# Pads in eight pools of a decoder-layer kernel: the two operands of most matrix multiplications get equal addresses modulo 256 bytes

## The chip, the core and the metric

The kernel runs on one core of a Trainium2 chip. Its engines work side by side, each through a queue of its own: TensorE (PE in the profile, with PEld for its loads of the stationary operand), VectorE (DVE), ScalarE (ACT), GpSimd (POOL) and SyncE (SP), which here issues most transfers. They share an on-chip memory of 128 partitions, the SBUF; the results of matrix multiplications land in a second memory, the PSUM. The metric is the device time of one execution in microseconds, as a median of runs.

## The reference

One layer of a decoder with 512 tokens and a width of 1024, all in float32. In short:

```
hn = rms_norm(x, g_mix);  z = hn @ w_in            # queries, keys, values, pool inputs, gates
A  = trailing-window pooling mixer                 # @ w_pool_out
B  = sparse attention: compressed + selected + window branches, sigmoid gated   # @ w_nsa_out
C  = cross-attention into mem (256 rows)           # @ w_x_out
x  = x + (sigmoid(g0)*A + sigmoid(g1)*B + sigmoid(g2)*C) @ w_o
h  = rms_norm(x, g_ffn)
# PEER: 8 heads, each picks 16 of 128*128 one-neuron experts by two half-queries
s  = scores of h @ w_peer_q against sub_keys;  ids, gate = two-stage top-16, softmax
x  = x + sum_k gate_k * gelu(h . u[ids_k]) * v[ids_k]
out = rms_norm(x, g_final)
```

## The kernel before, in words

**Numbers.** Each float32 factor `a` is held as two tiles: `a_hi`, a copy of `a` in the format `fp32r`, and `a_lo = a - a_hi`. A product is the sum of three matmuls, hi·hi, hi·lo and lo·hi. `split` (L132 to L134) makes the pair: ACT copies to the hi tile, DVE or POOL subtracts for the lo tile.

**One matmul has two operands in SBUF.** The *stationary* operand (128 columns, one LDWEIGHTS in the profile) is loaded into TensorE; the *moving* operand (64 to 512 columns) is then streamed through it. The profile names them in the order moving, stationary: `z<-hnh,wh` streams `hnh` through `wh`. While one matmul streams, the load for the next one runs beside it.

**The stages, in order of time** (us from the start of the span):

1. 0 to 40: memory keys and values (`mh`, `ml` against weights; 256 columns).
2. 40 to 250: the columns of `w_in` in tiles of 128 (`mm3_steps`, L161: `hnh`, `hnl` are moving, 512 columns, the weight tile `wh` or `wl` stationary), the values (L416, 280 columns), cross-attention (L454, L489) and its merge (`oxh`, `oxl`).
3. 240 to 515: sparse attention (L894, L926, L942 to L951) in an order of units, with the pool merge (`poolh`, `pooll`) and the next keys and queries between them in pieces of four matmuls.
4. 515 to 587: merge of the attention output (`onh`, `onl` and again `hnh`, `hnl`; 512 columns). 587 to 634: the projection `w_o` (L1156; the weights are moving, `mgh`, `mgl` stationary).
5. 635 to 745: the PEER queries (`q_mm`, L161: `hfh`, `hfl` moving, all 512 tokens).
6. From 635 on, the first layer of the experts (`hidden`, L161: 128 blocks `j` of 128 experts). It streams only the tokens 160 to 511 of `hfh`, `hfl`, so 352 columns, 24 matmuls a block: `p[:, X:NT]`, `x[:, k, t0 + X:T]` with `t0 = 128`, `X = 32`. 72 blocks (`LEAD`) run ahead, up to 1070 us, beside the retrieval of the expert numbers and the one-hot matmuls of the gates (L1453); their results go out to device memory.
7. 1074 to 1822: the last layer of the experts (`experts`, L1611). An iteration is one block: the 128 rows of `v` (two halves of 512 columns, hi and lo) are moving, the gated hidden values `wgh`, `wgl` are stationary: 3 token blocks x 3 products x 2 halves = 18 matmuls of 512 columns. The first 56 iterations also hold the 24 matmuls of `hidden`; the last 72 take the stored results. Beside it the 128 remaining tokens are done row by row: POOL gathers 256 rows of `u` and `v` (L1476), DVE multiplies them (L1490, L1496).

**What sets the order.** The schedule is manual: each engine works in program order. `weave` merges the experts' generator with the gathering one by given costs, `tiles` does so for attention.

**Pools and addresses.** A pool is a stack of tiles. Left pools grow from low addresses up, right pools from the top down, in the order in which they are opened. Tiles lie one behind the other in the order of the calls, and each start is rounded to 32 bytes. A tile that nobody reads (`name="pad"`) only moves what lies behind it (in a right pool: all the tiles of the pool, and the pools under it). One such pad stands in the kernel before: `wv2.tile([128, 216], F32, name="pad")` ahead of the expert weights.

Of the kernel before, what the change touches and what calls it, by code (L numbers as in the profile page):

```python
# [10 lines left out]
F32 = mybir.dt.float32  # L11
F32R = mybir.dt.float32r
# [12 lines left out]
KD = 8  # L25
# [85 lines left out]
def layer(ctx: ExitStack, tc: tile.TileContext, A: dict, out: bass.AP, dbg=None):  # L111
    nc = tc.nc
    v, s, g, pe = nc.vector, nc.scalar, nc.gpsimd, nc.tensor
# [6 lines left out]
    def sbuf(stack, name, side="left"):  # L120
        return stack.enter_context(tc.tile_pool(name=name, bufs=1, side=side, reuse_waits="tile"))
# [147 lines left out]
    rp = sbuf(rst, "rp", "right")  # L269
    acc = rp.tile([128, KD, T], F32, name="acc")  # L270
    poolh = rp.tile([128, 4, T], F32R, name="poolh")
    pooll = rp.tile([128, 4, T], F32R, name="pooll")
    mgp = sbuf(rst, "mg", "right")
    pms = ExitStack()
    pm = gfeed.pool = sbuf(pms, "pm", "right")
    xst = ExitStack()
    xa = sbuf(xst, "xa", "right")
    oxh = xa.tile([128, 4, T], F32R, name="oxh")
    oxl = xa.tile([128, 4, T], F32R, name="oxl")
    x2st = ExitStack()  # L280
    xk = sbuf(x2st, "xk", "right")
    Kh = xk.tile([128, 4, M], F32R, name="Kh")
# [113 lines left out]
    wv = sbuf(vst, "wv")  # L396
    WV = {}

    def wv_fetch(br):
        raw = wv.tile([128, KD * 280], F32, tag="vr", name="vr")  # L400
        nc.sync.dma_start(raw, A["w_v"][br])
        WV[br] = raw

    def wv_part(br):
        hi = wv.tile([128, KD, 280], F32R, tag="vh", name="vh")
        lo = wv.tile([128, KD, 280], F32R, tag="vl", name="vl")
        split(hi, lo, WV[br].rearrange("p (k n) -> p k n", n=280), v)
        WV[br] = (hi, lo)

# [362 lines left out]
    kqp = sbuf(ast, "kq")  # L772
# [2 lines left out]
    SC = [kqp.tile([128, 2, 4, 32], F32, name=f"sc{qp}") for qp in range(2)]  # L775
    for t_ in SC:
        g.memset(t_, NEG)

    def compress(gq, qp):

        def job():
            p = psum("z", [128, T])
            pc = p.rearrange("p (q r i c) -> p q r i c", q=2, r=4, i=2)
            sc = SC[qp]
            ns = [7 + 8 * (2 * qp + qi) for qi in range(2)]
            t_ = {}

            def steps():
                for qi in range(2):
                    qb = 2 * qp + qi  # L790
                    for r in range(4):
                        pe.matmul(pc[:, qi, r], Q[gq, r][:, qb * 128:(qb + 1) * 128], KC[:, gq],
                                  start=qi == 0 and r == 0, stop=qi == 1 and r == 3, skip_group_check=True)
                yield 0.9

            def add0():
                for qi, n in enumerate(ns):
                    j0 = 31 - n
                    v.tensor_tensor(sc[:, qi, :, 0:n], pc[:, qi, :, 0, 0:n], TTC[:, gq * 4:gq * 4 + 4, j0:j0 + n], op=OP.add)

            def add1():
                for qi, n in enumerate(ns):
                    v.tensor_tensor(sc[:, qi, :, 0:n], sc[:, qi, :, 0:n], pc[:, qi, :, 1, 0:n], op=OP.add)

            def top():
                t_["m"] = kqp.tile([128, 2, 4], F32, name="cnm")
                v.tensor_reduce(t_["m"], sc, axis=AX.X, op=OP.max)

            def sub():
                t_["e"] = kqp.tile([128, 2, 4, 32], F32, name="cex", bufs=2)  # L810
                v.tensor_tensor(t_["e"], sc, t_["m"][:, :, :, None].to_broadcast([128, 2, 4, 32]), op=OP.subtract)

            def exp():
                s.activation(t_["e"], t_["e"], AF.Exp)

            def total():
                t_["s"] = kqp.tile([128, 2, 4], F32, name="csm")
                v.tensor_reduce(t_["s"], t_["e"], axis=AX.X, op=OP.add)

            def inverse():  # L820
                v.reciprocal(t_["s"], t_["s"])

            def gated():
                v.tensor_tensor(t_["s"], t_["s"], gsig[:, 2 * qp:2 * qp + 2, gq * 4:gq * 4 + 4], op=OP.mult)

            def scaled():
                v.tensor_tensor(t_["e"], t_["e"], t_["s"][:, :, :, None].to_broadcast([128, 2, 4, 32]), op=OP.mult)

            def turned():
                PcT = [kqp.tile([128, 384], F32R, name=f"PcT{i}") for i in range(2)]  # L830
                pt = psum("tr", [128, 4, 128])
                for qi in range(2):
                    pe.transpose(pt[:, 1 - qi], t_["e"][:, qi].rearrange("p r c -> p (r c)"), ident)
                split(PcT[0][:, 0:256], PcT[1][:, 0:256], pt[:, 0:2].rearrange("p q t -> p (q t)"))
                for i in range(2):
                    s.activation(PcT[i][:, 256:384], f(PcT[i])[:, 0:128], AF.Copy)
                PC[gq, qp] = PcT

            TURN[gq, qp] = turned
            return p, steps(), [add0, add1], [top, sub, exp, total, inverse, gated, scaled]  # L840
        return job
# [235 lines left out]
    ep = sbuf(ctx, "ep")  # L1077
# [2 lines left out]
    mbx = ep.tile([128, X], F32, name="mbx")  # L1080
    HG = [ep.tile([128, NT], F32, name=f"hg{i}") for i in range(6)]
    idle = list(HG)

    lead_q = [s]

# [12 lines left out]
    n2 = sbuf(n2s, "n2")  # L1098
# [2 lines left out]
    X1 = [*(x1g[:, b] for b in range(GB)), *(x1n[:, b] for b in range(ND))]  # L1101
    iota16 = n2.tile([128, 16], F32, name="iota16")
    gf = n2.tile([128, D], F32, name="gf")
    src = A["iota128"]
    loads = [lambda b=b: nc.sync.dma_start(X1[b], A["x"][b * 128:(b + 1) * 128]) for b in range(NB)]
    loads.append(lambda: bcast_row(gf, A["g_ffn"]))
# [365 lines left out]
    ex_ = []  # L1472
# [92 lines left out]
    def experts():  # L1565
        acc_o.extend(psum(("S", "S", "tr", "tr", "o", "o")[i], [128, 512]) for i in range(2 * ND))
        for n in range(-1, 128):
            m = n + 1
            if m < 128:
                j = order[m]  # L1570
                if j >= LEAD:
                    U[m] = feed.take(("u", j))
                vfetch(m + 3)
                hfetch(m + 4)
                if m == 8:
                    bcast_row(gl, A["g_final"])
                if m == 100:
                    for b in range(GB, NB):
                        X1[b] = (X1B if b == GB
                                 else uf.tile([128, D], F32, tag="wr", name="wr", bufs=2))  # L1580
                        nc.sync.dma_start(X1[b], x1d[b - GB])
                if m % 8 == 4 and m + 4 < 128:
                    gload(m // 8 + 1)
                if j >= LEAD:
                    vpart(m)
                    yield 1.35
                    H[m] = hidden(U.pop(m))
                gh = GH.pop() if GH else ex_[0].tile([128, NT], F32, name="gh", bufs=2)
                idle.append(H[m])
                v.tensor_tensor(gh.rearrange("p (g t) -> p g t", t=UT), G[m // 8][:, :, m % 8 // 2, :, m % 2],  # L1590
                                H.pop(m).rearrange("p (g t) -> p g t", t=UT), op=OP.mult)
                if j < LEAD:
                    yield 1.0
                wh = WGH.pop() if WGH else ex_[0].tile([128, NT], F32R, name="wgh", bufs=3)
                wl = ex_[0].tile([128, NT], F32R, name="wgl", bufs=3)
                split(wh, wl, gh)
                if j < LEAD:
                    vpart(m)
                V[m] = (wh, wl, V[m])
                if j >= LEAD:  # L1600
                    yield 1.35
            if n < 0 or n == 126:
                continue

            ends = n == 127
            for b in range(ND):
                for k, hs in [(k, (half,)) for half in range(2) for k in (126, 127)] if ends else [(n, range(2))]:
                    wh, wl, vw = V[k]
                    for i, (a, c) in enumerate(((wh, vw[0]), (wl, vw[0]), (wh, vw[1]))):
                        for half in hs:  # L1610
                            pe.matmul(acc_o[2 * b + half], a[:, b * 128:(b + 1) * 128], c[:, half],  # L1611
                                      start=k == 0 and i == 0, stop=k == 127 and i == 2)
                    if ends and k == 127:
                        closing(GB + b, hs[0])
                        if b and hs[0] == 0:
                            finish(GB + b - 1)
                        if b and hs[0]:
                            for half in range(2):
                                output(GB + b - 1, half)
            V.pop(n)  # L1620
# [83 lines left out]
    gath = seq(*[gathered(b) for b in range(GB)])  # L1704
    ost2.close()
    wv2 = sbuf(hst, "wv2")
    wv2.tile([128, 216], F32, name="pad")
    vfetch(0)
    vfetch(1)
    gload(0)  # L1710
# [13 lines left out]
    X1B = ex.tile([128, D], F32, name="x1b")  # L1724
    bound_x()
    vfetch(2)
    seen = ep.tile([128, 1], F32, name="seen")
    g.tensor_copy(G[0][:, 0], own)
    g.tensor_copy(seen, VR[2][:, 0:1])
    weave((experts(), 2.7 * (128 - LEAD) + 1.0 * LEAD), (gath, 268 * GB))  # L1730
    finish(NB - 1)
    for half in range(2):
# [88 lines left out]
```

## Time and profile before

| | |
|---|---|
| time, median of 3 runs | 1832.12 us (1831.17 to 1832.64) |
| the profiled execution | 1831.29 us, its span 1829.5 us |
| TensorE, busy | 1805.9 us (99%), 10088 matmuls |
| VectorE, busy | 1361.5 us (74%) |
| ScalarE, busy | 836.7 us (46%) |
| GpSimd, busy | 765.6 us (42%) |
| moved by DMA | 446.00 MB, mean 244 GB/s |

A line of the groups reads: line, engine, operation, output<-inputs, shapes, count, busy us and mean ns of one, idle time before it and what ended it. Matmuls are pipelined: the *mean ns of one* runs from its start to its modelled end and is longer than the distance from one start to the next. What the stream costs is that distance. It is read from the timeline, where equal neighbours stand in one row: a row's start minus the start of the row before it, over the count of the row before it.

### The profile page before, as it was taken

The page shows a single profiled execution, that of the slowest core. Times are in us where ns is not written, and L with a number is a line of the kernel's source. Part 1 is how long each engine was busy: PE and PEld are TensorE (multiplying, and loading weights), DVE is VectorE, ACT ScalarE, POOL GpSimd, SP SyncE. Part 2 cuts the span into 40 slices and gives each one's busy share as a digit, 9 for nine tenths or more (in the row PEclk, how much of TensorE's full clock was granted, in tenths as well). Part 3 has the DMA queues.
Part 4 walks back from the last instruction along what each step waited for, and adds up shares of the span by engine and source line. Part 5 has one row for each costly group of instructions (what it writes and reads, how often), then busy time and mean ns, then how long its engine had stood idle before and what let it go on. Part 6 is the DMA issues. An engine that isn't in the chain of part 4 may idle for free.

```text
span 1829.5 us, 27951 instructions
## 1 busy us (share of the span) xinstructions
PE 1805.9 (99%) x10088; PEld 1584.9 (87%) x10088; DVE 1361.5 (74%) x2813; ACT 836.7 (46%) x1476; POOL 765.6 (42%) x597
## 2 busy tenths in 40 slices
PE   8999999999999999999999999999999999999998
PEld 7988888888888888999999988988988988888886
DVE  5453157766543479999989858998988998888886
ACT  6434267776642433554554543333333333333334
POOL 4323555555633233312222035666666664333320
PEclk9999999999999999999999999999999999999999
DMA  6225622112223432477999899999999999999992
GB/s 222 91 81 181 223 88 65 58 53 58 64 89 110 163 127 86 144 232 248 353 331 343 269 359 409 403 375 378 380 358 361 378 372 365 369 369 364 384 345 102
DMA packets 157276, 446.00 MB, mean 244 GB/s; under 512 B 16049, under 2 KB 61825, under 8 KB 154450
## 3 DMA queue, kind: packets, MB, share of 16 engines
q1 hardware_dynamic: 88194, 262.96, 40.1%
q0 software_dynamic: 41968, 152.14, 22.4%
q10 hardware_dynamic: 26976, 29.12, 4.8%
q8 instruction: 79, 1.29, 0.3%
q14 instruction: 59, 0.48, 0.1%
HBM read 402.15 MB, written 47.26 MB: 246 GB/s over the span
## 4 chain that ended last, share of the span: by engine, by line
PE 85%; DVE 5%; DMA 4%; ACT 3%; issue 1%; POOL 1%; ACTq 0%; DVEq 0%; SPq 0%; POOLq 0%
PE z L161 44%; PE S L1611 9%; PE o L1611 9%; PE tr L1611 9%; DMA ug<-in_u_rows_dram,ids 2%; PE S L894 1%; PE tr L926 1%; PE S L1156 1%; PE o L942 1%; DMA gd<-stg 1%; ACT pr L907 1%; PE o L416 1%; PE o L1239 1%; DVE pr L904 1%; PE z L1156 1%
## 5 line engine op out<-in xcount | busy, mean ns | idle before, releaser
L133 ACT ACTIVATE wh<-wr 128x1024 fp32r<-128x1024 f32 (+2 forms) x365 | 372.3, 1025 | 187.6 <-PE o L1611 47.6
L161 PE MATMUL z<-hfh,wh 128*128 128x352 f32 (+1 forms) x1136 | 376.0, 333 | 2.0 <-ACT wh L133 2.0
L134 DVE TENSOR_TENSOR wl<-wr,wh 128x1024 fp32r<-128x1024 f32 (+1 forms) x256 | 307.5, 1218 | 93.1 <-ACT wh L133 92.0
L134 POOL TENSOR_TENSOR wl<-wr,wh 128x1024 fp32r<-128x1024 f32 (+2 forms) x109 | 239.7, 2200 | 321.6 <-ACT wh L133 275.5
L161 PE MATMUL z<-hfl,wh 128*128 128x352 f32 (+1 forms) x1136 | 373.0, 330 | 0.0
L1476 POOL DMA_INDIRECT ug<-in_v_rows_dram,ids x128 | 175.3, 1370 | 208.7 <-DVE x1g L1496 191.9
L1476 POOL DMA_INDIRECT ug<-in_u_rows_dram,ids x128 | 190.9, 1492 | 111.5 <-DVE ug L1490 92.9
L161 PEld LDWEIGHTS z<-hfh,wh 128*128 128x128 f32 x1136 | 213.7, 188 | 10.2 <-ACT wh L133 2.9
L161 PEld LDWEIGHTS z<-hfl,wh 128*128 128x128 f32 x1136 | 213.7, 188 | 7.4
L161 PE MATMUL z<-hfh,wl 128*128 128x352 f32 (+1 forms) x1136 | 213.9, 330 | 0.2 <-DVE wl L134 0.2
L161 PEld LDWEIGHTS z<-hfh,wl 128*128 128x128 f32 x1136 | 188.6, 188 | 6.0 <-DVE wl L134 0.5
L1205 ACT ACTIVATE hg<-z 128x352 f32<-128x352 f32 x128 | 59.2, 462 | 268.0 <-PE z L161 265.4
L133 ACT ACTIVATE wgh<-gh 128x384 fp32r<-128x384 f32 x128 | 67.3, 526 | 240.0 <-DVE gh L1590 238.2
L1496 DVE SCALAR_TENSOR_TENSOR x1g<-ug,wgt,x1g 128x1024 f32<-128x1024 f32 x128 | 163.9, 1281 | 1.1
L1490 DVE SCALAR_TENSOR_TENSOR ug<-ug,hf 128x1024 f32<-128x1024 f32 x128 | 152.8, 1219 | 8.0 <-DMA ug<-in_u_rows_dram,ids 8.0
L161 PE MATMUL z<-hnh,wh 128*128 128x512 f32 x384 | 150.9, 393 | 0.0
L161 PE MATMUL z<-hnl,wh 128*128 128x512 f32 x384 | 150.4, 392 | 0.0
L1389 POOL DMA_INDIRECT ux<-in_u_rows_dram,idx x32 | 51.9, 1622 | 172.6 <-DVE ux L1397 168.7
L915 POOL TENSOR_SCALAR pr<-pr,sm,gsig 128x128 f32<-128x128 f32 (+3 forms) x128 | 78.1, 614 | 77.8 <-DVE sm L989 51.5
L134 DVE TENSOR_TENSOR wgl<-gh,wgh 128x384 fp32r<-128x384 f32 x128 | 71.6, 560 | 37.2 <-ACT wgh L133 37.2
L161 PE MATMUL z<-hnh,wl 128*128 128x512 f32 x384 | 99.2, 393 | 0.0
L930 DVE TENSOR_TENSOR PB<-tr,PB 128x128 fp32r<-128x128 f32 (+3 forms) x128 | 62.6, 489 | 49.2 <-ACT PB L929 48.6
(407 smaller groups left out, 3606.3 us busy)
## 6 DMA issues: line engine op xcount, KB each, us to landing
wr<-in_u_t_dram SPq DMA_DIRECT2D x128, 512.0 KB, 6.7
wr<-in_v_rows_dram SPq DMA_DIRECT2D x128, 512.0 KB, 8.8
wr<-in_w_z_dram SPq DMA_DIRECT2D x48, 512.0 KB, 3.6
gd<-stg ACTq DMA_DIRECT2D x11, 2048.0 KB, 15.0
hg<-hd SPq DMA_DIRECT2D x72, 176.0 KB, 8.4
gj<-gd SPq DMA_DIRECT2D x8, 1408.0 KB, 11.5
go<-gd SPq DMA_DIRECT2D x8, 1408.0 KB, 12.1
hd<-hg SPq DMA_DIRECT2D x61, 176.0 KB, 6.4
```

The lines of the kernel that those rows point to most:

```text
L133: s.activation(hi, src, AF.Copy)
L134: (eng or v).tensor_tensor(lo, src, f(hi), op=OP.subtract)
L161: pe.matmul(p, w[a][:, k], xs(x[b], k), start=k == 0 and a == 0 and b == 0, stop=k == nk - 1 and a == 1)
L915: g.tensor_scalar(pr[:, 0:n], pr[:, 0:n], sm, gsig[:, qb, c:c + 1], op0=OP.mult, op1=OP.mult)
L930: return lambda: v.tensor_tensor(lo, pt[:, 0:qb + 1], f(hi), op=OP.subtract)
L1156: pe.matmul(pos[half][b], (mgh, mgl)[a][:, k, b * 128:(b + 1) * 128], w[c][:, kk], start=k == 0 and a == 0 and c == 0, stop=k == 7 and c == 1)
L1205: s.activation(hg[:, X:], p[:, X:NT], AF.Gelu)
L1389: g.indirect_dma_start(out=XR[k], out_offset=None, in_=A["u_rows"], in_offset=bass.IndirectOffsetOnAxis(ap=idx[:, k:k + 1], axis=0))
L1476: g.indirect_dma_start(out=row, out_offset=None, in_=src, in_offset=bass.IndirectOffsetOnAxis(ap=ids[:, b, k:k + 1], axis=0))
L1490: v.scalar_tensor_tensor(row, row, 1.0, hf[:, b], op0=OP.mult, op1=OP.mult, accum_out=act[:, m:m + 1])
L1496: v.scalar_tensor_tensor(X1[b], rows.pop(m), wgt[:, m - 128:m - 127], X1[b], op0=OP.mult, op1=OP.add)
L1611: pe.matmul(acc_o[2 * b + half], a[:, b * 128:(b + 1) * 128], c[:, half], start=k == 0 and i == 0, stop=k == 127 and i == 2)
```

## The change

Nothing is computed in another way. Pads are added in eight pools or moved, the value weights of the first stages get a row stride of 320 instead of 280 columns, and the small tile `seen` moves from the pool `ep` into the place of the old pad in `wv2`.

```
+    rp.tile([128, 8], F32, name="pad")                  # behind pooll
+    xa.tile([128, 8], F32, name="pad")                  # behind oxl
+    gap = [56]
     def wv_part(br):
-        hi = wv.tile([128, KD, 280], F32R, tag="vh", name="vh")
-        lo = wv.tile([128, KD, 280], F32R, tag="vl", name="vl")
+        if gap:
+            wv.tile([128, gap.pop()], F32, name="pad")
+        hi = wv.tile([128, KD, 320], F32R, tag="vh", name="vh")[:, :, 0:280]
+        lo = wv.tile([128, KD, 320], F32R, tag="vl", name="vl")[:, :, 0:280]
...
             def turned():
+                if spare:                                # spare = [56]
+                    kqp.tile([128, spare.pop()], F32, name="pad")
                 PcT = [kqp.tile([128, 384], F32R, name=f"PcT{i}") for i in range(2)]
...
     HG = [ep.tile([128, NT], F32, name=f"hg{i}") for i in range(6)]
+    ep.tile([128, 32], F32, name="pad")
...
     gf = n2.tile([128, D], F32, name="gf")
+    n2.tile([128, 48], F32, name="pad")
...
                 if m == 100:
+                    ex_[0].tile([128, 8], F32, name="pad")
...
-    wv2.tile([128, 216], F32, name="pad")
+    seen = wv2.tile([128, 192], F32, name="seen")
...
-    seen = ep.tile([128, 1], F32, name="seen")
-    g.tensor_copy(seen, VR[2][:, 0:1])
+    g.tensor_copy(seen[:, 0:1], VR[2][:, 0:1])
```

What it does to the addresses, read from the two built programs: start of the moving and of the stationary operand modulo 256, and their distance (moving minus stationary, modulo 256). Steps along a tile are multiples of 256 bytes but for the values before, whose rows of 280 floats walk through all multiples of 32.

| matmuls (moving, stationary) | columns | count | before | after |
|---|---|---|---|---|
| L161 `hnh`/`hnl`, w | 512 | 1152 | 192, 192: 0 | same |
| L161 `onh`/`onl`, w (with L154) | 512 | 192 | 192, 192: 0 | same |
| L1611 v rows, `wgh`/`wgl` | 512 | 2304 | 192, 224: 224 | 192, 192: 0 |
| L161 `hfh`/`hfl`, query weights (with L154) | 512 | 384 | 96, 192: 160 | 192, 192: 0 |
| L1156 `w_o`, `mgh`/`mgl` | 512 | 192 | 192 or 160, 224: 224 or 192 | 192, 192: 0 |
| L161 `oxh`/`oxl`, w | 512 | 96 | 0, 192: 64 | 192, 192: 0 |
| L161 `poolh`/`pooll`, w | 512 | 96 | 224, 192: 32 | 192, 192: 0 |
| L942, L945, L951 `PB`, `PcT` against values | 256 | 384 | 224, 192: 32 | 192, 192: 0 |
| L161, L350 `mh`/`ml`, w | 256 | 192 | 64 or 192 | 0 |
| L454 `Kh`/`Kl`, q | 256 | 48 | 0, 192: 64 | 192, 128: 64 |
| L416 value weights, `hnh`/`hnl` | 280 | 192 | all eight | 192, 192: 0 |
| **L161 `hfh`/`hfl`, first expert layer (with L154)** | **352** | **3072** | **224, 192: 32** | **64, 192: 128** |

The order of the instructions is the same on every engine. Waits differ at one place, the start of attention, where tiles now lie over other, older tiles. On SP, which issues the transfers, the bias rows `TT` of the first heads stood so before (`brow` are the older bias rows, `wr` the raw weights; DMAHW are transfers that must have landed):

```order
L849 DMA brow<-shr 128x512 [waits DMAHW0_49]
L78 DMA wr<-in_w_z_dram 128x1024 [waits DMAHW1_49,Pool_49]
L78 DMA wr<-in_w_z_dram 128x1024 [waits DMAHW4_49,Pool_49]
L875 DMA TT<-shr 128x512 [waits DMAHW5_49]
L875 DMA TT<-shr 128x512 [waits DMAHW2_49,PE_49]
L875 DMA TT<-shr 128x512 [waits DMAHW3_49]
L875 DMA TT<-shr 128x512
```

and stand so now:

```order
L858 DMA brow<-shr 128x512 [waits DMAHW0_49]
L78 DMA wr<-in_w_z_dram 128x1024 [waits DMAHW1_49,Pool_49]
L78 DMA wr<-in_w_z_dram 128x1024 [waits DMAHW4_49,Pool_49]
L884 DMA TT<-shr 128x512 [waits DMAHW5_49,DMAHW3_49]
L884 DMA TT<-shr 128x512 [waits PE_49]
L884 DMA TT<-shr 128x512 [waits DMAHW2_49]
L884 DMA TT<-shr 128x512
```

The same landings are waited for, one of them a row earlier and one a row later. In the same way DVE's first write of `PB` (L930, now L939) waits for two landings more, of loads issued in the same stretch.

More of the change, by code (lines that the diff above doesn't have):

```diff
@@ L777, in layer @@
         g.memset(t_, NEG)
+    spare = [56]
     def compress(gq, qp):
```

## The prediction

> **What bounds the kernel now.** First the page's engine shares and clock, then the waits of TensorE over the whole span:
>
> ```profile
> PE 1805.9 (99%) x10088; PEld 1584.9 (87%) x10088; DVE 1361.5 (74%) x2813; ACT 836.7 (46%) x1476; POOL 765.6 (42%) x597
> PEclk9999999999999999999999999999999999999999
> PE S L894 <- DVE nm L904: 2.8, 7, 0.8
> PE z L315 <- DMA grow<-in_g_mem_dram: 2.4, 1, 2.4
> PE z L161 <- ACT wh L133: 2.0, 1, 2.0
> ```
>
> TensorE is busy 99% of the span at an undisturbed clock, and its longest waits sum to 2 or 3 us each. A busy TensorE alone would prove little, since the ends of matmuls are modelled. So I read what the stream of matmuls costs from one start to the next, in the timeline of TensorE. First two stretches where the operands lie equal modulo 256 (distance 0):
>
> ```profile
> 547.37 1.98 PE L161 MATMUL z<-hnh,wl 128*128 128x512 f32 x8
> 549.18 0.39 PE L161 MATMUL z<-onh,wh 128*128 128x512 f32 x1
> ...
> 552.81 1.98 PE L161 MATMUL z<-onh,wl 128*128 128x512 f32 x8
> 554.62 0.39 PE L161 MATMUL z<-hnh,wh 128*128 128x512 f32 x1
> ```
>
> Eight matmuls of 512 columns take 549.18 - 547.37 = 1.81 us, 226 ns each, and so do the eight of `onh`. Now the PEER queries (distance 160) and one whole iteration of the last expert layer (distance 224):
>
> ```profile
> 650.03 2.03 PE L161 MATMUL z<-hfh,wl 128*128 128x512 f32 x8
> 651.91 1.05 PE L1239 MATMUL o<-skt,qT 128*128 128x128 f32 x8
> ...
> 1523.84 0.63 PE L1611 MATMUL S<-wh,wgh 128*128 128x512 f32 x2
> 1528.04 0.63 PE L1611 MATMUL S<-wh,wgh 128*128 128x512 f32 x2
> ```
>
> The same shape takes 1.88 / 8 = 235 ns in the queries, and 4.20 us / 18 = 233.3 ns in the expert layer. Nothing waits in either. That is 7 ns more per matmul, with the address distance as the difference named in front. Other traffic doesn't sort them as well. Four stretches, with engines and DMA beside them:
>
> ```profile
> core 0: us, PE busy (x) PEld busy (x) DVE busy (x) ACT busy (x) POOL busy (x), PEclk, DMA share, GB/s
> 640.00:760.00 120.00, 119.75 (x610) 101.92 (x609) 105.90 (x740) 40.90 (x59) 47.41 (x20) 1.00 0.31 107
> 760.00:1070.00 310.00, 308.63 (x2413) 305.49 (x2411) 269.52 (x322) 166.84 (x250) 60.18 (x43) 1.00 0.87 294
> 1240.00:1510.00 270.00, 270.00 (x1413) 242.55 (x1412) 242.04 (x309) 100.12 (x134) 169.65 (x109) 1.00 0.97 370
> 1520.00:1820.00 300.00, 300.00 (x1287) 241.34 (x1286) 252.09 (x302) 117.40 (x156) 87.43 (x74) 1.00 0.89 334
> ```
>
> The queries are slow at a DMA share of 0.31, the expert layer at 0.89.
>
> **The change part by part.** Counts are those of the groups kept apart by shape (the last layer has nine such rows, the 352 columns three, the queries three and 24 matmuls of L154):
>
> ```profile
> L161 PE MATMUL z<-hfh,wh 128*128 128x352 f32 x1016 | 327.3, 324 | 2.0 <-ACT wh L133 2.0
> L1611 PE MATMUL S<-wh,wgl 128*128 128x512 f32 x256 | 81.0, 397 | 0.0
> L161 PE MATMUL z<-hfh,wh 128*128 128x512 f32 x120 | 48.7, 406 | 0.0
> L161 PE MATMUL z<-onh,wh 128*128 128x512 f32 x56 | 21.8, 389 | 0.0
> L1156 PE MATMUL o<-wh,mgh 128*128 128x512 f32 x16 | 6.3, 396 | 0.0
> L454 PE MATMUL S<-Kh,qh 128*128 128x256 f32 x16 | 4.4, 277 | 0.0
> L942 PE MATMUL o<-PB,V 128*128 128x256 f32 x256 | 44.5, 281 | 0.0
> L350 PE MATMUL o<-wh,mh 128*128 128x256 f32 x32 | 8.0, 285 | 0.6 <-DVE Vx L134 0.6
> ```
>
> *Last expert layer.* 9 x 256 = 2304 matmuls, 233.3 to 226.7 ns: 2304 x 6.6 = 15.2 us. A stream doesn't reach its pace at once. After twelve matmuls of `oxh`, `oxl` the next 24 of `hnh`, `hnl` run from here to there:
>
> ```profile
> 179.12 0.40 PE L161 MATMUL z<-oxh,wh 128*128 128x512 f32 x1
> ...
> 181.88 0.40 PE L161 MATMUL z<-hnh,wh 128*128 128x512 f32 x1
> ...
> 187.37 0.40 PE L161 MATMUL z<-oxh,wh 128*128 128x512 f32 x1
> ```
>
> 5.49 us / 24 = 228.8 ns: about 0.05 us lost against 226.7, though their distance is 0. In the last layer 55 iterations follow on 24 matmuls of 352 columns; I take 0.04 us each, 2.2 us. Left: 13.0 us. Bounds: 0 (addresses are not the cause) and 15.2.
>
> *Queries.* 3 x 120 + 24 = 384 matmuls, 235 to 226.7: 3.2 us, less 0.04 for each of 16 fresh starts: 2.5.
>
> *Projection `w_o`.* 192 matmuls whose mean from start to end is 396 against 389 of `onh`: 7 ns each, 1.3 us.
>
> *Cross-attention merge and pool merge.* `oxh`: 2.76 us / 12 = 230 ns, so 96 x 3 = 0.3 us, and the 0.05 us of each of eight following `hnh` tiles goes: 0.4. The pool merge runs in pieces of four, too short to settle: 0.2. Together 0.9.
>
> *256 and 280 columns.* The best rows stand at 277 (L454), others at 281 to 285; 576 matmuls x 4 to 8 ns bounds it at 2.3 to 4.6 us. But the 192 of `mh`, `ml` lie in the first 40 us, where loads set the pace, and `PB` is cut up by transposes: I take 0.6, bounds 0 and 4.6.
>
> *352 columns: the open term.* 3072 matmuls go from distance 32 to 128. Now they cost, in an iteration of the mixed part:
>
> ```profile
> 1300.92 1.44 PE L161 MATMUL z<-hfh,wl 128*128 128x352 f32 x8
> 1302.20 0.63 PE L1611 MATMUL S<-wh,wgh 128*128 128x512 f32 x2
> ```
>
> 1.28 / 8 = 160 ns. No row has this shape at another distance. From both sides: 512 columns show a step of 6.6 ns between distance 0 and 224, so 3072 x 6.6 = 20 us more, or 20 us less if 160 already holds such a step. The nearest row is the shape's own. Two readings pull apart. Per column 226.7 / 512 is 0.443 ns, which for 352 is 156, so 160 leaves room below. But from start to end 352 takes 324, which is 65 less than 389 for 160 columns fewer, 0.41 ns a column, so 160 looks like a settled stream already. I take 160, with both ends for the range.
>
> *What costs nothing.* `vl` is split with rows of 320; the two splits lie under other work. The moved waits at the start of attention ask for loads of `brow`, the last issued at 225.1 us and at most 4.4 us in landing; the `TT` loads are issued from 234.48 us on:
>
> ```profile
> L849 SPq DMA_DIRECT2D brow<-shr x16: 320/423/433, 191.3 to 225.1; - x16
> DMA to landing us min/median/max: 3.7/4.1/4.4
> 234.48 7.72 SPq L875 DMA_DIRECT2D TT<-shr  x4
> ```
>
> Uncovered, one landing would hold up SP's next loads by 4.4 us, and attention with them.
>
> *Can the others follow?* DVE is busy 242 of 270 us in the mixed part and 252 of 300 in the last, where an iteration would shrink from 4.20 to 4.08 us and DVE's 3.53 us per iteration still fit. In the mixed part 8.04 us become about 7.97, against DVE's 7.21. DMA has the least room, 370 GB/s at a share of 0.97, but TensorE waits for nothing there. I deduct nothing; the bound is that all 9 us of the mixed part and its start are lost.
>
> Sum: 13.0 + 2.5 + 1.3 + 0.9 + 0.6 + 0 = 18.3 us. The profiled execution took 1831.29 us, 0.83 below the median; on the median, 1832.12 - 18.3 = 1814 us.
>
> **The rivals.**
>
> *B, the 352 columns gain too.* Their moving operand now starts on a multiple of 64 bytes (64 instead of 224), as do both operands of all quick rows (192, 192). At 0.443 ns per column, 4 ns each, 12 us more: 1802; with the whole step, 1794.
>
> *C, the 352 columns lose a little.* `oxh`, 64-byte aligned at distance 64, pays 230 against 226.7. 3072 x 3 = 9 us back: 1823.
>
> *D, slower: the first expert layer pays what the last one saves.* If distance alone counts, 128 is as far from 0 as can be, and 352 columns pay the 6.6 ns of distance 224: 20 us, in the stretch 635 to 1511. From 18.3 us / 3072 = 6.0 ns per matmul on the change loses: 1834. Against it: 352 at distance 32 is nowhere irregular, while 512 columns at distance 32 (`poolh`, 398 from start to end by its group) are slow like the rest; so distance does not act on both alike.
>
> *E, addresses don't matter* and 226 and 235 differ by what runs beside them: 1832. For it: the quick rows all lie before 590 us, where DVE is half idle. Against it: `w_o` at 396, in the same quiet part.
>
> ```profile
> 560.00:610.00 50.00, 50.00 (x219) 40.87 (x219) 14.35 (x15) 15.79 (x22) 21.57 (x9) 1.00 0.46 150
> L161 PE MATMUL z<-poolh,wh 128*128 128x512 f32 x32 | 12.7, 398 | 0.3 <-ACT th L753 0.3
> ```
>
> [...]
>
> **How the numbers follow.** A, as summed, 352 within 1.3 ns of 160: 42%, 1810 to 1818. B: 30%, 1794 to 1810. C: 14%, 1818 to 1828. D: 6%, 1832 to 1836. E, or gains that DVE and the transfers swallow: 8%, 1828 to 1833. The measurement tells about 0.2% (3.7 us) from no change. Faster by that: A, B and C, 86%; within: E, 8%; slower: D, 6%. Eight in ten are held by all of A, most of B and C: 1796 to 1828.
>
> **What would show it.** Right: rows of eight `hfh,wl` with 512 columns at 1.81 us instead of 1.88, iterations after 1520 us at 4.08 instead of 4.20, L1611's mean at 389 or 390, and 352 columns still 1.28 us for eight. B, C or D show in that last figure (1.23, 1.30, 1.33). E: all four as before. If TensorE gets a new wait on `wgh` or `wh` in 1074 to 1510, others set the pace. The forecast is wrong if the 352 columns move by more than 4 ns, or if L1611 doesn't.

## The result, and the profile after

The changed kernel takes 1820.98 us (median of 5 runs, 1820.77 to 1823.89) against 1831.78 beside it: a ratio of 0.9947, interval 0.9932 to 0.9961. It is faster by 10.8 us, where 18.3 were forecast. Taken again later beside other kernels it took 1821.07, ratio 0.9949 (0.9935 to 0.9963).

First the engine shares of its page:

```profile
PE 1795.0 (99%) x10088; PEld 1591.6 (87%) x10088; DVE 1361.4 (75%) x2813; ACT 837.0 (46%) x1476; POOL 767.7 (42%) x597
```

TensorE is as full as before, so the gain is in the pace of its stream. The timeline of TensorE, a query tile and two iterations of the last expert layer:

```profile
649.98 1.98 PE L161 MATMUL z<-hfh,wl 128*128 128x512 f32 x8
651.80 1.06 PE L1250 MATMUL o<-skt,qT 128*128 128x128 f32 x8
...
1517.80 0.62 PE L1623 MATMUL S<-wh,wgh 128*128 128x512 f32 x2
1521.88 0.62 PE L1623 MATMUL S<-wh,wgh 128*128 128x512 f32 x2
```

Eight query matmuls take 1.82 us instead of 1.88, and an iteration 4.08 instead of 4.20: 18 matmuls at 226.7 ns. Both are what the prediction asked for. The 352 columns are not. Two places of the same timeline, the first behind the one-hot matmuls of the gates, the second in the mixed part:

```profile
858.43 0.62 PE L1464 MATMUL S<-ob,oa 128*128 128x128 f16 x8
858.86 0.41 PE L161 MATMUL z<-hfh,wh 128*128 128x352 f32 x1
...
861.60 1.50 PE L161 MATMUL z<-hfh,wl 128*128 128x352 f32 x8
862.94 0.33 PE L161 MATMUL z<-hfh,wh 128*128 128x352 f32 x1
...
1405.47 1.43 PE L161 MATMUL z<-hfh,wl 128*128 128x352 f32 x8
1406.74 0.63 PE L1623 MATMUL S<-wh,wgh 128*128 128x512 f32 x2
```

1.34 us for eight in the one (167 ns each), 1.27 in the other (158.8), where it had been 1.28 (160.0) everywhere. The groups kept apart by shape show the same, and a small loss that was not forecast (from start to end the three rows had 324, 397 and 281 ns):

```profile
L161 PE MATMUL z<-hfh,wh 128*128 128x352 f32 x1016 | 329.2, 327 | 0.0
L1623 PE MATMUL S<-wh,wgl 128*128 128x512 f32 x256 | 79.8, 391 | 0.0
L951 PE MATMUL o<-PB,V 128*128 128x256 f32 x256 | 44.9, 282 | 0.0
```

By stage, from the start of the first matmul of each (us):

| stretch | before | after | difference |
|---|---|---|---|
| to the first block of 352 columns | 635.3 | 635.6 | +0.2 |
| PEER queries | 102.5 | 100.0 | -2.5 |
| from there to the first gate matmul | 111.3 | 114.5 | +3.1 |
| to the first matmul of the last layer | 220.4 | 224.6 | +4.3 |
| mixed part | 436.5 | 429.8 | -6.7 |
| last layer alone | 310.7 | 301.9 | -8.8 |

These add up to -10.4, the change in the start of the last matmul (the first block of 352 columns, 5.2 us before and after, stands between the first two rows). The three stretches with 512 columns win 18; the two between them, run ahead and gates, give 7.4 back. In the first of these two stands a wait that the kernel before didn't have (0.2 us there). The waits of TensorE from 742 to 855 us (in total, times, longest):

```profile
PE z L161 <- DVE wl L134: 1.9, 1, 1.9
```

Its timeline at that place:

```profile
768.03 0.32 PE L161 MATMUL z<-hfl,wh 128*128 128x352 f32 x1
770.23 1.79 PE L161 MATMUL z<-hfh,wl 128*128 128x352 f32 x8 [1.88 <-DVE wl L134]
```

And busy time and granted clock in two windows, the wait and what follows:

```profile
core 0: us, PE busy (x) PEld busy (x) DVE busy (x) ACT busy (x) POOL busy (x), PEclk, DMA share, GB/s
768.00:770.20 2.20, 0.35 (x3) 0.06 (x1) 2.20 (x8) 2.17 (x3) 0.00 (x0) 1.00 0.38 143
771.50:774.70 3.20, 3.20 (x12) 3.20 (x12) 3.17 (x6) 1.52 (x2) 0.00 (x0) 0.50 0.93 349
```

The queries end 2.5 us earlier, but DVE, which selects the top 16 there and splits `wl` in between, is busy 2.20 of 2.20 us and doesn't follow. TensorE stands for 1.9 us, and soon after gets half its clock (0.50 over the 3.2 us shown), in which 11 matmuls start 293 ns apart.

### The profile page after: what moved, and what is told of

Same layout as the page of the kernel before. It is cut to its first block, busy times and chain, and to the rows that moved or that the text cites. A ratio compares the mean times of both kernels' runs of the same rounds, so it can differ in the third digit from the quotient of the medians.

```text
span 1819.2 us, 27952 instructions
## 1 busy us (share of the span) xinstructions
PE 1795.0 (99%) x10088; PEld 1591.6 (87%) x10088; DVE 1361.4 (75%) x2813; ACT 837.0 (46%) x1476; POOL 767.7 (42%) x597
## 4 chain that ended last, share of the span: by engine, by line
PE 83%; DVE 10%; ACT 3%; DMA 2%; POOL 1%; issue 1%; DVEq 0%; SPq 0%; ACTq 0%; POOLq 0%
PE z L161 42%; PE S L1623 9%; PE tr L1623 9%; PE o L1623 9%; PE S L903 2%; PE tr L935 1%; PE o L951 1%; DMA ug<-in_u_rows_dram,ids 1%; PE o L422 1%; PE S L1167 1%; DVE si L1268 1%; DVE s L1264 1%; DVE si L1261 1%; PE S L1464 1%; PE tr L1464 1%
## 5 line engine op out<-in xcount | busy, mean ns | idle before, releaser
L161 PE MATMUL z<-hfh,wh 128*128 128x352 f32 (+1 forms) x1136 | 377.2, 334 | 0.0
L161 PE MATMUL z<-hfl,wh 128*128 128x352 f32 (+1 forms) x1136 | 373.9, 330 | 0.0
L161 PEld LDWEIGHTS z<-hfh,wh 128*128 128x128 f32 x1136 | 214.0, 188 | 7.0 <-ACT wh L133 0.6
L161 PEld LDWEIGHTS z<-hfl,wh 128*128 128x128 f32 x1136 | 214.1, 188 | 6.3
L161 PE MATMUL z<-hfh,wl 128*128 128x352 f32 (+1 forms) x1136 | 214.7, 331 | 1.9 <-DVE wl L134 1.9
L161 PEld LDWEIGHTS z<-hfh,wl 128*128 128x128 f32 x1136 | 189.8, 188 | 7.1 <-DVE wl L134 2.4
L161 PE MATMUL z<-hnh,wh 128*128 128x512 f32 x384 | 150.8, 393 | 0.0
L161 PE MATMUL z<-hnl,wh 128*128 128x512 f32 x384 | 150.3, 391 | 0.0
L939 DVE TENSOR_TENSOR PB<-tr,PB 128x128 fp32r<-128x128 f32 (+3 forms) x128 | 62.6, 489 | 49.7 <-ACT PB L938 49.0
L161 PE MATMUL z<-hnh,wl 128*128 128x512 f32 x384 | 99.1, 392 | 0.0
```

Of the source, the lines that this page charges most:

```text
L161: pe.matmul(p, w[a][:, k], xs(x[b], k), start=k == 0 and a == 0 and b == 0, stop=k == nk - 1 and a == 1)
L939: return lambda: v.tensor_tensor(lo, pt[:, 0:qb + 1], f(hi), op=OP.subtract)
```

## The experiments

The spacings below are distances from one start to the next, from the trace records of each class of matmuls. Times of a class are sums of these distances. Each ratio is to the kernel before run beside the experiment (medians 1830.3 to 1831.8 us).

**Bare streams.** Nothing but matmuls: eight moving tiles `m`, each 32 bytes further on, against one weight tile `w` (and `w2`, 64 bytes further on), in the order of `mm3_steps`, a dozen matmuls of another shape in between:

```
def stream(mv, n, groups=2, w=w):
    for _ in range(groups):
        p = z[turn[0] % 4][:, 512 - n:512]
        ...
        for a in range(2):
            for k in range(8):
                for b in range(2 - a):
                    pe.matmul(p, w[:, 8 * a + k], mv[:, (k + 4 * b) % 8, 0:n], ...)
...
for n in (352, 256):
    for d in range(0, 256, 32):
        stream(m[d], n)
        short(m[0], 512, 12)
```

> Leaves the layer out: only streams of 48 matmuls from seven distances between moving and stationary start modulo 256 bytes, in columns of 512, 352 and 256, with 12 matmuls of another shape between them; nothing else runs. Theory 1, the addresses alone set the pace: 512 columns take 226.7 ns at distance 0 and 229 to 235 elsewhere (234 at 160, 233 at 224, 229 to 231 at 64); 352 columns take 160.0 at distance 32 and at 128 either 166.7 or 158.5, and what came before them (512 or 64 columns) decides which; 256 columns take 120 at distance 0 and 117 to 118 at 32; the same distance from another absolute start (w2) gives the same pace. Rival, what runs beside the matmuls sets the pace: with nothing beside them all 512-column streams take 226.7, all 352-column streams the same number, and all 256-column streams the same number.

(Eight distances, in fact.) The busy times of the bare streams, in the columns of the windows above:

```profile
20.00:446.00 426.00, 422.71 (x2401) 386.44 (x2399) 0.69 (x1) 18.47 (x20) 0.00 (x0) 1.00 0.00 1
```

Some of them in their timeline (512 columns at distance 224; 352 at 32 and 128; 256 at 0 and 32; 512 at 0 against `w2`):

```profile
112.28 11.36 PE L147 MATMUL z<-m,w 128*128 128x512 f32 x48
123.48 2.08 PE L154 MATMUL z<-m,w 128*128 128x352 f32 x12
...
135.83 7.85 PE L147 MATMUL z<-m,w 128*128 128x352 f32 x48
143.51 2.92 PE L154 MATMUL z<-m,w 128*128 128x512 f32 x12
...
167.22 7.77 PE L147 MATMUL z<-m,w 128*128 128x352 f32 x48
174.83 2.91 PE L154 MATMUL z<-m,w 128*128 128x512 f32 x12
...
208.90 5.92 PE L147 MATMUL z<-m,w 128*128 128x256 f32 x48
214.65 2.91 PE L154 MATMUL z<-m,w 128*128 128x512 f32 x12
217.40 5.76 PE L147 MATMUL z<-m,w 128*128 128x256 f32 x48
223.00 2.91 PE L154 MATMUL z<-m,w 128*128 128x512 f32 x12
...
348.63 11.14 PE L147 MATMUL z<-m,w 128*128 128x512 f32 x48
359.61 2.09 PE L154 MATMUL z<-m,w 128*128 128x352 f32 x12
```

At a DMA share of 0.00 and with DVE idle, 512 columns still take 11.20 / 48 = 233.3 ns at distance 224. All distances, as means over the second half of each stream:

| distance | 0 | 32 | 64 | 96 | 128 | 160 | 192 | 224 |
|---|---|---|---|---|---|---|---|---|
| 512 columns, ns | 226.7 | 233.3 | 233.3 | 233.3 | 232.7 | 234.4 | 233.3 | 233.3 |
| 352 columns, ns | 160.0 | 160.0 | 160.0 | 162.2 | 158.3 | 160.0 | 160.0 | 160.0 |
| 256 columns, ns | 120.0 | 116.7 | 117.8 | 120.0 | 120.0 | 118.5 | 117.8 | 118.3 |

Against `w2`, tried with 512 and 352 columns, distances 0, 32, 128 and 192 give the same within 0.6 ns. (The 352 columns at distance 0 took 160.0 behind 352 columns and 161.1 behind 512; at the other distances they took the same behind 512 columns and behind 64.) So for these two widths the distance sets the pace, not the absolute start and not the traffic, and the rival falls. For 256 columns no second start was tried, and one class in the layer speaks against the distance alone: `Kh`, `Kl` against `q` (L454, now L460) stand at distance 64 before and after, since both starts moved together. Yet behind the 512 columns of L489 (now L495) they took 113.3 ns each before and take 117.6 now. Why stays open. Two parts of theory 1 missed: 512 columns at 64 take 233.3, not 229 to 231, and 352 at 128 ran at 158.3 alone, with no 166.7 behind either lead. What puts them into 166.7 was open.

**The parts of the change, one by one.** `last_only` is the kernel before with one pad of the eight:

```
                 if m == 100:
+                    ex_[0].tile([128, 8], F32, name="pad")
```

> The kernel before with one pad alone, the one that moves wgh and wgl by 32 bytes. Theory 1, each class of matmuls is paid by its own distance and the gains add up: the last layer goes from 233.4 to 227.3 ns a matmul, 14.2 us; the 352 columns stay at 160.0 and the queries at 234; 1831.8 - 14.2 = 1817.6 (1816 to 1819). Rival, a faster last layer disturbs the rest (the 352 columns in the mixed part, DVE, the transfers), which is where 7 us of the forecast went: 1821 to 1825.

`first_alone` is the kernel before with `hfh`, `hfl` moved alone; the other two pads only keep `w_o` and the rows of `v` where they were:

```
     idle = list(HG)
+    ep.tile([128, 24], F32, name="pad")
...
+    n2.tile([128, 40], F32, name="pad")
...
-    wv2.tile([128, 216], F32, name="pad")
+    wv2.tile([128, 192], F32, name="pad")
```

> The kernel before with the move of hfh and hfl by 96 bytes alone; everything else stands where it stood. Theory 1, this part of the change is a loss: queries 2.6 us less, the 352 columns 6 us more where they fall into the 166.7 ns pace beside the gates, sum + 3.4 (+ 2 to + 8, more if the slower 512 columns ahead of them, at distance 224, put the mixed part into 166.7 too). Rival, the 352 columns are slowed by the rest of the change (other tiles over other tiles, other times): they stay at 160.0 or go to 158.5 throughout, and the time falls by 2.6 or by 7.

`first_back` is the changed kernel with this one move undone:

```
-    ep.tile([128, 32], F32, name="pad")
+    ep.tile([128, 8], F32, name="pad")
...
-    n2.tile([128, 48], F32, name="pad")
+    n2.tile([128, 72], F32, name="pad")
...
-    seen = wv2.tile([128, 192], F32, name="seen")
+    seen = wv2.tile([128, 216], F32, name="seen")
```

> The changed kernel with hfh and hfl moved back down by 96 bytes, everything else where the change put it: queries at distance 160, 352 columns at 32. Theory 1, the address of hfh makes the 352 columns fall into two paces: they return to 160.0 everywhere (498 us instead of 504), the queries lose 2.6 us again, sum 1821.0 - 6.0 + 2.6 = 1817.6 (1816.5 to 1819). Rival, the two paces come from what is beside or ahead of the 352 columns in the changed kernel: they stay at 158.5 and 166.7, and the queries alone cost 2.6: 1823.6.

| | time, us | ratio to before (interval) | last layer, us | queries | 352 columns |
|---|---|---|---|---|---|
| before | 1831.78 | | 538.3 | 91.2 | 498.2 |
| the change | 1820.98 | 0.9947 (0.9932 to 0.9961) | 524.1 | 88.6 | 504.2 |
| `last_only` | 1817.70 | 0.9934 (0.9922 to 0.9947) | 525.1 | 91.2 | 497.4 |
| `first_alone` | 1835.37 | 1.0022 (1.0013 to 1.0031) | 537.5 | 88.6 | 507.8 |
| `first_back` | 1817.02 | 0.9926 (0.9913 to 0.9939) | 526.8 | 91.2 | 497.0 |

The timeline of `last_only`, two iterations of the last layer:

```profile
1514.54 0.61 PE L1612 MATMUL S<-wh,wgh 128*128 128x512 f32 x2
1518.62 0.61 PE L1612 MATMUL S<-wh,wgh 128*128 128x512 f32 x2
```

The timeline of `first_alone`, 352 columns beside the gates:

```profile
903.65 1.50 PE L161 MATMUL z<-hfh,wl 128*128 128x352 f32 x8
904.99 0.33 PE L161 MATMUL z<-hfh,wh 128*128 128x352 f32 x1
```

The same place in the timeline of `first_back`:

```profile
902.32 1.44 PE L161 MATMUL z<-hfh,wl 128*128 128x352 f32 x8
903.60 0.32 PE L161 MATMUL z<-hfh,wh 128*128 128x352 f32 x1
```

One pad brings nearly the whole gain of the last layer (13.2 of 14.2 us, 4.08 us an iteration); by the medians that is more than the eight together. The move of `hfh` alone makes the kernel slower by 0.13% to 0.31%: 55 of its 128 blocks run at 166.7 (1.34 us for eight), with all the other tiles in their old places. Undone in the changed kernel, all blocks run at 160.0 again (1.28). Both rivals fall: the last layer disturbs nothing, and the two paces come with the address of `hfh`, not with the rest of the change.

**256 columns.** `narrow_back` is the changed kernel with two pads undone:

```
-    spare = [56]
+    spare = []
...
     ml = mt_.tile([128, KD, M], F32R, name="ml")
+    mt_.tile([128, 48], F32, name="pad")
```

> The changed kernel with the pad ahead of PcT left out and a pad behind ml added, so that the 384 matmuls of 256 columns in attention stand at distance 32 and the 192 of the memory at 64 and 192 again. Theory 1, 256 columns are slower at distance 0: PB from 119.1 to 117.6 ns, 0.7 us, and the memory from 119.7 to 116.9, 0.6 us if the loads of the first 40 us don't hide it: 1819.6 to 1820.3. Rival, the 1.5 ns are what runs beside them: 1821.0, the spacing unchanged.

The attention matmuls go from 119.1 back to 117.6 ns (46.1 to 45.5 us), the memory from 119.7 to 117.3 (27.0 to 26.3); the time is 1819.83, ratio 0.9944 (0.9932 to 0.9955). The spacing settles it against the rival, and the bare streams agree; the 1.3 us themselves are below what the times can tell. `both_back` has the edits of `narrow_back` and `first_back` together.

> The changed kernel with both parts undone that lost: hfh and hfl 96 bytes lower as before, the 256 columns of attention and of the memory at distances 32, 64 and 192 as before. Theory 1, the terms add: first_back's 1817.0 less 1.2 (0.6 for PB, 0.6 for the memory if the loads don't hide it) = 1815.8 (1815 to 1817). Rival, the 256 columns lie beside waits: 1817.0, as first_back.

It took 1817.01, ratio 0.9921 (0.9909 to 0.9934), the median of `first_back`. In its profile both sums of 256 columns are back at 45.5 and 26.3 us, and the first block of 352 columns still starts no earlier than in `first_back` (635.6 against 634.8 us). So the expectation of another 1.2 us isn't borne out; that these columns are hidden by the loads of the first stages is possible and wasn't settled.

**What puts 352 columns into the slow pace.** Bare streams again, 48 matmuls at distance 128 and then at 32, behind leads as the layer has them: three or four transposes, 8 or 64 f16 matmuls (`oa`), and these with one or two more matmuls behind them:

```
elif lead == 1:
    onehot(64)
elif lead == 2:
    onehot(8)
elif lead == 3:
    onehot(64)
    short(m[0], 64, 1)
...
stream(m[d], 352)
```

> Leaves the layer out: streams of 48 matmuls of 352 columns at distance 128 and then at 32, each behind another lead: three or four transposes, 8 or 64 f16 matmuls as in the gates, these with one or two matmuls of 64, 128 or 512 columns behind them. Theory 1, at distance 128 the stream has two paces that hold themselves, and what stands ahead decides which: behind the gates' 64 f16 matmuls it locks at 166.7, behind 512 columns it cycles at 158.5, behind transposes either; at 32 every lead gives 160.0. Rival, the 166.7 needs the traffic of the layer beside it: every stream at 128 runs at 158.5 here.

The timeline, at distance 128 behind 64 f16 matmuls, behind the same and one of 64 columns, behind three and behind four transposes, and at distance 32 behind 64 f16:

```profile
32.40 3.84 PE L165 MATMUL z<-oa 128*128 128x128 f16 x64
36.05 8.24 PE L147 MATMUL z<-m,w 128*128 128x352 f32 x48
44.13 0.63 PE L165 MATMUL z<-oa 128*128 128x128 f16 x8
...
56.30 0.28 PE L154 MATMUL z<-m,w 128*128 128x64 f32 x1
56.41 7.85 PE L147 MATMUL z<-m,w 128*128 128x352 f32 x48
64.11 3.84 PE L165 MATMUL z<-oa 128*128 128x128 f16 x64
...
75.68 0.49 PE L172 MATMUL z<-ident,raw 128*128 128x128 f32 x3
75.92 7.85 PE L147 MATMUL z<-m,w 128*128 128x352 f32 x48
83.61 0.60 PE L172 MATMUL z<-ident,raw 128*128 128x128 f32 x4
83.97 8.24 PE L147 MATMUL z<-m,w 128*128 128x352 f32 x48
92.05 3.85 PE L165 MATMUL z<-oa 128*128 128x128 f16 x64
...
150.79 7.93 PE L147 MATMUL z<-m,w 128*128 128x352 f32 x48
158.56 0.63 PE L165 MATMUL z<-oa 128*128 128x128 f16 x8
```

Without the first distance of each (244 to 251 ns), 8.08, 7.70, 7.69, 8.08 and 7.77 us are 166.7, 158.4, 158.4, 166.6 and 160.0 ns a matmul by the records. At distance 128 the f16 lead (three of three, 8 or 64 long) and four transposes (tried once) lock the stream at 166.7 for all its 48 matmuls; three transposes (three of three), one or two short f32 matmuls, or 512 columns leave it at 158.3. At 32 all eleven leads give 160.0. Theory 1 holds: both paces, 158.3 and 166.7, come with the layer left out.

**The lead changed in the layer.** `entry` puts a matmul of 64 columns between gates and block, and behind the transposes of `turn_sel`:

```
+    ahead = []
     def hidden(w, then=None, **order):
         p = psum("z", [128, T])
+        if ahead:
+            ahead.clear()
+            pe.matmul(p[:, X:X + 64], w[0][:, 0], hfh[:, 0, 0:64], start=True, stop=True)
...
     def gates(u, oa, ob, then=None):
...
+        ahead.append(u)
...
     def turn_sel(b):
...
+        ahead.append(b)
...
     last_store = gates(units[-1], *pend)
+    ahead.clear()
```

> The changed kernel with 14 more matmuls of 64 columns (hfh against the block's own weights, into the PSUM columns that the block then overwrites), one ahead of the first block of hidden behind each set of one-hot matmuls and behind each three transposes of turn_sel. Theory 1, what stands ahead of a stream of 352 columns at distance 128 chooses between 166.7 and 158.5, as in the bare streams: the 45 blocks of 24 at 166.7 go to 158.5, 45 x 24 x 8.2 = 8.9 us, for 14 x 0.1 = 1.4 us: 1821.0 - 7.4 = 1813.5 (1812 to 1815.5). Rival, in the layer it is the traffic beside the gates (one-hot masks written by DVE, stores) that holds 166.7: the blocks stay at 166.7 and the time is 1822.

`entry_narrow` adds the edits of `narrow_back`, and `after_again` is the changed kernel beside them.

> As entry, and the 256 columns of attention and memory back at their distances of before. Theory 1: entry's time less 0.7 to 1.3: 1812.5 (1811 to 1814.5), faster than the kernel before, the changed one and the one with hfh moved back (1817.0). Rival, as with hfh moved back, where the same undoing moved the median by nothing: equal to entry.

> The changed kernel itself, beside the two others on one chip. All theories: 1821 (1820 to 1824); its spread of 3 us between executions comes, by theory 1, from blocks of 352 columns that take one pace or the other, and the two kernels beside it, with one pace everywhere, spread less than 2 us; by the rival all three spread alike.

`entry_gates` is `entry_narrow` without the lines in `turn_sel` and without the last `ahead.clear()`.

> As entry_narrow, but the matmuls of 64 columns stand behind the gates alone, and behind all 12 sets of one-hot matmuls (the last had none), none behind the transposes of turn_sel. Theory 1, each lead has its pace: behind the gates no block stays at 166.7, also not the five around 1060 us, 1.0 us; behind the transposes, where the added matmul itself put 7 and more blocks into 166.7, they go back to 158.4 in most stretches, 0.6 to 2.5 us: 1815.3 - 1.6 to 3.5 = 1812 to 1814. Rival, the pace behind such a lead is chance from execution to execution: locked blocks remain in other places and the median stays at 1815 to 1816.5.

| | time, us (range) | ratio to before (interval) | blocks at 166.7 | blocks at 158 to 159 |
|---|---|---|---|---|
| `after_again` | 1821.07 (1819.45 to 1821.35) | 0.9949 (0.9935 to 0.9963) | 48 | 78 |
| `entry` | 1816.32 (1815.01 to 1817.79) | 0.9927 (0.9913 to 0.9940) | 13 | 114 |
| `entry_narrow` | 1815.29 (1812.44 to 1817.12) | 0.9914 (0.9901 to 0.9928) | 22 | 106 |
| `entry_gates` | 1814.24 (1813.59 to 1817.87) | 0.9916 (0.9902 to 0.9929) | 12 | 115 |

The timeline of `entry_gates` behind the second set of gates (L1217 is the added matmul):

```profile
878.55 0.28 PE L1217 MATMUL z<-hfh,wh 128*128 128x64 f32 x1
878.66 0.41 PE L161 MATMUL z<-hfh,wh 128*128 128x352 f32 x1
...
881.28 1.43 PE L161 MATMUL z<-hfh,wl 128*128 128x352 f32 x8
882.54 0.32 PE L161 MATMUL z<-hfh,wh 128*128 128x352 f32 x1
```

1.26 us for eight instead of 1.34: behind every added matmul at the gates the block, and those after it, run at 158.3. The rival of `entry` falls. Its 1813.5 was not reached since 13 blocks stayed: by the trace (46 - 13) x 24 x 8.2 ns = 6.5 us come back, the 14 added matmuls cost 1.6, and 1821.0 - 4.9 = 1816.1 lies near the measured 1816.32. Five of the 13 stand behind the last gates, which the edit had left out, seven behind transposes, and one block has a wait in it. `entry_narrow` lies 1.0 us below `entry`, but missed its range of 1811 to 1814.5, and with 22 locked blocks against 13 the two can't show what the 256 columns are worth.

In `entry_gates` the five are gone. The 12 left all stand behind the three transposes of `turn_sel`, and there its expectation failed: two of the three stretches, from 796 and from 840 us, are locked without an added matmul, so it wasn't the added matmul alone that locked them in `entry_narrow`. Two executions of the changed kernel differ there as well. From 827.6 us on, behind the same three transposes, the profile of `after_again` shows:

```profile
830.23 1.43 PE L161 MATMUL z<-hfh,wl 128*128 128x352 f32 x8
831.50 0.32 PE L161 MATMUL z<-hfh,wh 128*128 128x352 f32 x1
```

1.27 us for eight, where the first profile of the changed kernel has 1.34 at the same place (830.34 to 831.68). So behind these transposes the lead doesn't decide, and the rival of `entry_gates`, a pace that changes from execution to execution, fits the traces. The time doesn't settle it: 1814.24 lies between the two ranges. It is the lowest median of all, its interval below that of the changed kernel; the simpler `last_only`, `first_back` and `both_back` can't be told from it.

The three kernels do not spread as expected (1.9 us for `after_again`, 2.8 for `entry`, 4.7 for `entry_narrow`). But the two with added matmuls didn't have one pace everywhere, so this was no test of it. The kernel before, with all its blocks at 160.0, spreads over 3.0 us in the nine executions beside them, so two paces aren't needed for such a spread. Its cause stays open.

Waits for `wl` near 770 us are in every profile with `hfh` in its new place. The timeline of `entry` there:

```profile
769.68 1.55 PE L161 MATMUL z<-hfh,wl 128*128 128x352 f32 x8 [1.89 <-DVE wl L134]
774.88 1.54 PE L161 MATMUL z<-hfh,wl 128*128 128x352 f32 x8 [1.11 <-DVE wl L134]
```

Here the clock was not halved (1.00 from 770.0 to 774.7 us), and TensorE ran into a second wait for DVE instead. The delays beyond 160 ns at this place sum to 3.3 us in `entry` and to 3.5 in the changed kernel. So DVE's splits set the time there, and the halved clock cost little of its own.

## Why the prediction was right, and where it was wrong

The forecast "faster" held, and 1820.98 lies in the range of 1796 to 1828; the likeliest case, 1810 to 1818, was missed by 3 us. The sum was 8 us too high, and the range held it because it had been kept wide for the 352 columns. The terms against the trace:

| term | forecast, us | measured |
|---|---|---|
| last expert layer | 13.0 | 14.2 |
| queries | 2.5 | 2.6 |
| `w_o` | 1.3 | 0.5 |
| merges and pool | 0.9 | 0.7 |
| 256 and 280 columns | +0.6 | -1.2 |
| 352 columns | 0 | -6.0 |
| all else | 0 | -0.5 |
| sum | 18.3 | 10.3 |

**512 columns: right.** 233.3 to 226.7 was the right step, its cause is the distance, as the bare streams show without any traffic (226.7 ns at distance 0, 232.7 to 234.4 at the seven others, at a DMA share of 0.00 and with DVE busy for 0.69 of 426 us), and rival E fell with it. The deduction of 0.04 us for each fresh start was about twice too high: of 15.2 us 14.2 came. `w_o` did go from 233.2 to 227.2 ns, but 0.6 us more of waits lie within it in this execution.

**352 columns: the step that failed.** "I take 160" was the term that was wrong, and the text had named it as the open one. By the prediction's own sign, 352 columns moving by more than 4 ns, it failed in 46 of the 128 blocks. No case described what came. Rival B's gain is there, with a smaller size (80 blocks at 158 to 159, 2.9 us). Rival D's 6.6 ns are there too (166.7 - 160.0 = 6.7, in 46 blocks, 7.4 us), so "the first layer pays what the last one saves" was true for a third of the blocks. Waits, the one at 770 us above all, bring 1.5 more: -2.9 + 7.4 + 1.5 = 6.0. The time fell into the range of rival C by luck: its reason, a constant 3 ns, isn't the one, and the 230 ns of `oxh` that it went by are a run of 12 matmuls, while the bare stream of 512 columns at distance 64 settles at 233.3. The rows of before could not have shown this: at distance 32 the shape took 160.0 ns behind all eleven leads tried.

**256 columns: wrong in sign.** The prediction carried the rule of 512 columns, distance 0 is best, to a width that no row showed at 0. In the bare streams 256 columns take 120.0 ns there, more than at 32 (116.7).

**"Can the others follow?" was asked in the wrong places.** The mixed part and the last layer were looked at, and they did follow. The stretch behind the queries was not, though DVE's 105.90 of 120 us stood in a quoted row. So the queries' 2.5 us came, and were given back 30 us later: the first gate matmul starts at 855.2 us, 0.8 later than before. How much of that is DVE and how much the 166.7 ns between 828 and 840 us wasn't taken apart. In `first_back`, with slow queries and 160.0, it starts at 854.0.

## What to carry to other kernels

Measure the pace of a stream, start to start, for every shape that an alignment moves: equal addresses were best here for 512 columns (226.7 ns against 232.7 to 234.4) and among the slowest for 256 (120.0 against 116.7 to 120.0). Change such addresses one tile at a time, since one pad of eight did as much here as all of them (1817.70 us against 1820.98). And when a stage gets quicker, look at the engine that feeds the stage behind it, not only at the stage itself.

## What the runs showed of the hardware that was not expected

- A stream of 352 columns at distance 128 showed two paces, 158.3 and 166.7 ns, and kept either for all 48 matmuls of a bare stream and for up to 192 in the layer (from 797 us on: 158.3 in the changed kernel, 166.7 in `entry_gates`). Behind f16 matmuls it was 166.7 each time; one matmul of 64 columns behind those, 0.1 us, made it 158.3 each time. Behind the three transposes of `turn_sel` either came, with the added matmul and without it. Why, the traces don't tell.
- Of the three widths only 512 columns were quickest at distance 0 (226.7 ns). 256 columns took 120.0 there and 116.7 at 32. For 352 columns 0 (behind 352 columns) and five other distances were alike at 160.0, and 128 had 158.3 in the same streams.
- Behind the 1.88 us without a matmul near 770 us in the changed kernel the granted clock fell to 0.50 from 771.35 to 774.75 us; in the 3.40 us ahead (767.90 to 771.30) TensorE was busy for 1.52 at a clock of 1.00. In `entry` a gap as long, 1.89 us, was followed by the full clock (1.00 from 770.0 to 774.7 us). What decides between the two, these traces don't tell.
